# Ten of eleven row tiles of each half of a down projection through seven products, the plain parts moved ahead of the fourth product

## The chip, the cores and the metric

The kernel runs on one core of a Trainium2 chip. The metric is the device time of one execution in microseconds (us); the median of a few runs counts. Engines are named as in the profile: PE is the matrix engine, DVE the vector engine, ACT the scalar engine, POOL the GpSimd engine, SP the engine that issues most DMAs. A measurement of this kernel tells a difference from no change at about 0.2%, that is 2.2 us.

## The reference, cut to what matters

Two layers of a bidirectional encoder over 512 tokens with a model width of 1024. The change lies in the last line of each layer, the down projection with `w_down` (2816 x 1024).

```python
D_MODEL = 1024; SEQ = 512; DEPTH = 2; D_FF = 2816
def reference(...):
    for l in range(DEPTH):
        h = rmsnorm(x, mix_norm[l])
        ...                                   # attention, pooling and gating mixers
        x = x + jnp.einsum('bsn,nd->bsd', mix, w_o[l])
        h = rmsnorm(x, ffn_norm[l])
        g = jnp.einsum('bsd,df->bsf', h, w_gate[l])
        u = jnp.einsum('bsd,df->bsf', h, w_up[l])
        x = x + jnp.einsum('bsf,fd->bsd', jax.nn.silu(g) * u, w_down[l])
    return rmsnorm(x, final_norm)
```

## The kernel before

**Precision.** Every product of two float32 tiles is three matmuls: each operand is split into a high part (an ACT copy that rounds to the short type) and a low part (a DVE subtraction of the high part), and `mm` issues high x high, high x low, low x high. For weights `split` makes one `wu` tile of both parts out of a loaded 128x1024 tile `wr` (or `raw`); there are three `wu` buffers, so a split starts when the third `wu` before it has been used up on PE. For the left operand `halved` makes the two `xp` tiles.

**Seven products.** The activation is cut in two halves of 256 tokens (`i`) and two halves of the 2816 columns (`s`), the weight in two halves of rows (`h`) and two halves of 512 output columns (`s`). A product of 2x2 blocks by 2x2 blocks takes seven block products in place of eight (the Strassen-Winograd scheme). `products` issues them, `sum_of` builds the left operands (sums of activation blocks, tile names `xs` and `ac`), `operand` builds the right ones. The right operand of products 5, 6 and 4 is a running sum kept in `chain[b]`: W11, then + W12 (product 5), + W22 (product 6), + W21 (product 4). An addition to it is either a DVE addition of a second loaded tile (`wr<-wr,wr` in the profile) or `add_loaded`, a DMA issued from POOL that adds while it lands. Here W12 and W22 are added by DVE, W21 by DMA; product 7 has a DMA addition of its own (W22 onto a loaded W12). Product 3 uses the W22 tile that was loaded for product 6.

**Tiling.** Each half of the 2816 columns has eleven tiles of 128. Eight of them go through the seven products: `b` runs over four pairs of tiles, a "unit" here is one product and one pair: one 128x1024 weight split and twelve 128x512 matmuls (2 token blocks `j` x 2 tiles `kk` x 3). The last three tiles of each half are multiplied plainly in `rest`: `rest(1, ...)` for the second 512 output columns, `rest(0, ...)` for the first, each with three weight tiles, all three `wu` buffers, and 18 matmuls for each of four blocks of 128 tokens. The accumulating PSUM banks are `reg["z"]`, `reg["y"]`, `reg["x"]`, two each; `rest(1)` borrows two more, `spare`.

**Order.** The program order in `down` is product 1, 5, 6 and 3 interleaved by `b`, 2, 7, then `rest(1)`, product 4, `rest(0)`. A recording layer (`Program`) then places every instruction: `order` walks a list of ready instructions with planned times, `LEAD_FF = 100` lets loads and first uses of a buffer start up to 100 matmuls ahead of their place in the program. All instructions are emitted from one line, so the profile shows L493 for nearly all of them; they are told apart by the tile names.

**Ends.** A finished block of 128 tokens by 512 columns goes to `settle`. In layer 0 that is `back`: four PE transposes into a bank of tag `b` (two such banks, `spare` takes them too) and a DVE addition into `res`; `next_inputs` then prepares layer 1. In layer 1 it is `finish`: a square with a row sum (ACT), a gain (DVE), a power (POOL), two scalings (ACT and DVE) and the output DMAs.

Of the kernel before, what the change touches and what calls it, by code (L numbers as in the profile page):

```python
# [19 lines left out]
P = 128  # L20
# [59 lines left out]
def dn_unit(h, s, b):  # L80

    return 74 + (h * 8 + s * 4 if h < 2 else 16 + s * 3) + b
# [416 lines left out]
def encoder(ctx: ExitStack, tc: tile.TileContext, wts, xT, pos, cols, sgn, fin, cst, rc, out):  # L499
# [204 lines left out]
    for l in range(DEPTH):  # L704
# [560 lines left out]
        for c in range(3):  # L1265
# [3 lines left out]
            for mat in range(2):  # L1269
# [4 lines left out]
                def consume(src, j, i, s, c=c, w=w, nf=nf, mat=mat, stash=stash):  # L1274
# [25 lines left out]
                    for f in range(0, nf, 2):  # L1300
                        n = min(2, nf - f)
                        g, at = (s, 0) if f == 0 else ("both", s)
                        if g not in act:
                            act[g] = upool.tile([P, 2, T], F32, tag="u", name=nm("ac"), bufs=NU)
# [7 lines left out]
                        nc.scalar.copy(  # L1312
                            out=act[g][:, at : at + n, i * HALF : (i + 1) * HALF],
                            in_=ps[:, : n * HALF].rearrange("p (f q) -> p f q", q=HALF),
                        )
# [126 lines left out]
        sums = [None, None]  # L1442

        def sum_of(p, c):
            x11, x21, x12, x22 = (act[i, s, c] for s in range(2) for i in range(2))
            if p == 1:
                return x11
            if p == 2:
                return x12
            if p == 4:  # L1450
                return x22
            if p == 7:
                return x21
            if p == 5:
                sums[c] = upool.tile([P, 4, HALF], F32, tag="u", name=nm("xs"), bufs=NU)
# [10 lines left out]
        def operand(p, b):  # L1466
# [16 lines left out]
            chain["22"] = raw  # L1483
            add(chain[b][:], chain[b][:], raw[:])
            return chain[b]
# [3 lines left out]
        def products(ps_, due=None):  # L1489

            xs = {}
            for b in range(4):
                for p in ps_:
                    if b % 2 == 0:
                        xs[p] = halved(sum_of(p, b // 2))
                    xh, xl = xs[p]
                    wu = split(operand(p, b), U, nc.vector)
                    for j in range(2):
                        for kk in range(2):
                            k = 2 * b + kk  # L1500
                            js = slice(j * P, (j + 1) * P)
                            ws = slice(kk * T, (kk + 1) * T)
                            mm(
                                reg[REGION[p]][j][:], xh[:, k % 4, js], xl[:, k % 4, js], wu[:, 0, ws], wu[:, 1, ws],
                                p in OPENS and k == 0, k == 7,
                            )
                if due and b == 0:
                    settle(*due)

        KREST = [(1, 0), (1, 1), (0, 0), (0, 1), (0, 2), (1, 2)]  # L1510
        rest_parts = {}

        def rest_part(n):
            s, f = KREST[n]
            g = s if f < 2 else "both"
            if g not in rest_parts:
                m = U
                hi, lo = (upool.tile([P, 2, T], F32R, tag="u", name=nm("xp"), bufs=NU) for _ in range(2))
                nc.scalar.activation(flat(hi)[:, :m], flat(act[g])[:, :m], AF.Copy)
                add(flat(lo)[:, :m], flat(act[g])[:, :m], f32(flat(hi)[:, :m]), ALU.subtract)  # L1520
                rest_parts[g] = hi, lo
            return [x[:, f if f < 2 else s] for x in rest_parts[g]]

        def rest(h, targets, after):

            wus = [weights(l, dn_unit(2, h, b)) for b in range(3)]
            due = []
            for i, (banks, opens) in enumerate(targets):
                for j in range(2):
                    for k in range(6):  # L1530
                        xh, xl = rest_part(k)
                        t = 2 * i + j
                        js = slice(t * P, (t + 1) * P)
                        ws = slice(k % 2 * T, (k % 2 + 1) * T)
                        mm(
                            banks[j][:], xh[:, js], xl[:, js], wus[k // 2][:, 0, ws], wus[k // 2][:, 1, ws],
                            opens and k == 0, k == 5,
                        )
                    if due:
                        settle(*due.pop())  # L1540
                    due.append(after(i, j))
            return due.pop()
# [43 lines left out]
        def after0(i, j):  # L1586
            if i == 0:
                y = a1[j]
                add(y[:], reg["x"][j][:], y[:])
            else:  # L1590
                y = tmp()
                if last:
                    add(cols4(y[:]), cols4(reg["z"][j][:]), rows(2 + j, 0))
                else:
                    nc.scalar.copy(out=y[:], in_=reg["z"][j][:])
            return y, 2 * i + j, 0

        settle(*rest(0, [(reg["x"], False), (reg["z"], False)], after0))
# [19 lines left out]
def _pack(p):  # L1618
# [3 lines left out]
    for l in range(DEPTH):  # L1622
# [38 lines left out]
        for h in range(2):  # L1661
            for s in range(2):
                row += [wd[h, :8, :, s].transpose(1, 0, 2).reshape(P, -1)]
        for s in range(2):
            rest = [wd[h, 8 + f, :, s] for h, f in ((1, 0), (1, 1), (0, 0), (0, 1), (0, 2), (1, 2))]
            row += [np.stack(rest).transpose(1, 0, 2).reshape(P, -1)]
# [50 lines left out]
```

## Time and profile before

| | |
|---|---|
| median of 3 runs | 1096.61 us (1095.69 to 1096.83) |
| the profiled execution | 1096.24 us |
| its span, first to last instruction | 1094.5 us |
| mean granted clock of PE | 0.996 of full |
| PE busy | 1072.2 us, 98% of the span |
| DVE busy | 864.9 us, 79% |
| ACT busy | 649.7 us, 59% |
| POOL busy | 174.9 us, 16% |

The profiled execution lies within the three runs; what lies around its span is 1.74 us. Busy time is a share over stages with different limits, so the stages are read apart below.

### The profile page before, as it was taken

The numbers are of one execution on the slowest core, as the hardware profiler recorded it, in microseconds if no ns is written. First come the engines' busy times: TensorE is split into PE (matmuls) and PEld (weight loads), VectorE is DVE, ScalarE is ACT, GpSimd is POOL, SyncE is SP. The second block draws the span as 40 slices with busy tenths as digits, with TensorE's granted clock in tenths as the row PEclk, the third lists the DMA queues.
The fourth block names the chain that finished last, engine by engine and source line by source line (L and its number), as shares of the span: only waits on it lengthen the run. The fifth ranks groups of instructions, "written<-read, shape, count | busy, mean of one in ns | idle before, by whom it ended". The sixth has DMA issues, their size and how long they took to land.

```text
span 1094.5 us, 14564 instructions
## 1 busy us (share of the span) xinstructions
PE 1072.2 (98%) x5324; PEld 902.9 (82%) x5324; DVE 864.9 (79%) x1193; ACT 649.7 (59%) x993; POOL 174.9 (16%) x201
## 2 busy tenths in 40 slices
PE   9999899999999999999999999999999999999997
PEld 7787688888888899888887877888888889998885
DVE  7679996897877778995556898959977867799963
ACT  6357784775565556663443678747655655666632
POOL 0317430101001100030001263301001001100201
PEclk9999999999999999999999999999999999999999
DMA  6344313656545557392142533153767446563922
GB/s 214 101 119 117 104 39 128 219 153 135 155 130 120 122 132 248 114 235 80 60 132 67 140 99 88 58 229 99 187 141 169 109 117 142 130 219 102 259 64 96
DMA packets 45672, 146.90 MB, mean 134 GB/s; under 512 B 6000, under 2 KB 6256, under 8 KB 45600
## 3 DMA queue, kind: packets, MB, share of 16 engines
q1 hardware_dynamic: 35216, 112.24, 31.4%
q0 software_dynamic: 9808, 32.67, 17.0%
q10 hardware_dynamic: 576, 1.05, 0.3%
q8 instruction: 42, 0.69, 0.3%
q14 instruction: 30, 0.25, 0.1%
HBM read 135.33 MB, written 2.23 MB: 126 GB/s over the span
## 4 chain that ended last, share of the span: by engine, by line
PE 89%; DVE 4%; ACT 4%; DMA 1%; issue 1%; POOL 1%; POOLq 0%; SPq 0%; ACTq 0%; DVEq 0%
PE ps L493 89%; DVE u L493 2%; ACT t L493 1%; ACT u L493 1%; DMA wr<-in_wts 1%; DVE wu L493 1%; DVE s L493 1%; ACT wu L493 1%; DVE t L493 0%; POOL t L493 0%; DMA colt<-in_cols 0%; POOL z L493 0%; ACT vm L493 0%; DVE vz L493 0%; DVE wr L493 0%
## 5 line engine op out<-in xcount | busy, mean ns | idle before, releaser
L493 PE MATMUL ps<-wu,xp 128*128 128x512 f32 (+1 forms) x2976 | 657.7, 380 | 1.8 <-DVE wu L493 1.1
L493 PEld LDWEIGHTS ps<-wu,xp 128*128 128x128 f32 x2976 | 545.9, 188 | 92.8 <-DVE wu L493 2.3
L493 ACT ACTIVATE wu<-wr 128x1024 fp32r<-128x1024 f32 (+1 forms) x224 | 225.0, 1007 | 200.1 <-PE ps L493 163.5
L493 DVE TENSOR_TENSOR wu<-wr,wu 128x1024 fp32r<-128x1024 f32 (+1 forms) x224 | 257.9, 1154 | 89.6 <-ACT wu L493 88.5
L493 PE MATMUL ps<-u,wu 128*128 128x512 f32 x972 | 238.1, 397 | 2.8 <-DVE wu L493 2.1
L493 PEld LDWEIGHTS ps<-u,wu 128*128 128x128 f32 x972 | 180.1, 190 | 41.8 <-DVE wu L493 4.0
L493 POOL DMA_DIRECT2D wr<-in_wts x64 | 55.7, 978 | 553.0 <-DVE wr L493 276.6
L493 PE MATMUL ps<-u,u 128*128 128x256 f32 (+2 forms) x516 | 109.0, 349 | 5.2 <-ACT vm L493 1.7
L493 ACT ACTIVATE wu<-raw 128x1024 fp32r<-128x1024 f32 (+3 forms) x66 | 63.1, 959 | 65.5 <-PE ps L493 33.5
L493 PEld LDWEIGHTS ps<-u,u 128*128 128x128 f32 (+1 forms) x516 | 75.9, 190 | 21.0 <-DVE u L493 4.5
L493 ACT COPY t<-ps 128x512 f32<-128x512 f32 (+3 forms) x124 | 62.2, 502 | 49.3 <-PE ps L493 47.9
L493 DVE TENSOR_TENSOR wu<-raw,wu 128x1024 fp32r<-128x1024 f32 (+3 forms) x59 | 67.4, 1146 | 26.6 <-ACT wu L493 26.0
L493 DVE TENSOR_TENSOR wr<-wr,wr 128x1024 f32<-128x1024 f32 (+1 forms) x64 | 73.6, 1152 | 5.5 <-DMA wr<-in_wts 5.1
L493 DVE TENSOR_TENSOR u<-ps,u 128x512 fp32r<-128x512 f32 (+1 forms) x104 | 70.2, 683 | 6.1 <-ACT u L493 5.4
L493 DVE TENSOR_TENSOR t<-ps,t 128x512 f32<-128x512 f32 (+2 forms) x92 | 50.1, 566 | 24.6 <-PE ps L493 19.8
L493 ACT ACTIVATE u<-ps 128x512 fp32r<-128x512 f32 (+1 forms) x104 | 61.2, 595 | 12.1 <-PE ps L493 10.7
L493 ACT ACTIVATE t<-ps,s 128x512 f32<-128x512 f32 x64 | 43.9, 688 | 11.7 <-DVE s L493 11.2
L493 POOL TENSOR_SCALAR t<-t,s 128x512 f32<-128x512 f32 x55 | 38.4, 704 | 59.2 <-DVE s L493 48.4
L493 PE MATMUL ps<-ident,t 128*128 128x128 f32 x288 | 42.9, 274 | 0.8 <-DVE s L493 0.6
L493 DVE TENSOR_REDUCE s<-ps 128x1 f32<-128x512 f32 x64 | 42.9, 679 | 0.5 <-PE ps L493 0.2
L493 PEld LDWEIGHTS ps<-ident,t 128*128 128x128 f32 x288 | 34.2, 140 | 11.0 <-issue 3.2
L493 DVE TENSOR_TENSOR res<-ps,res 128x512 f32<-128x512 f32 x40 | 27.5, 686 | 18.9 <-PE ps L493 18.7
(130 smaller groups left out, 807.7 us busy)
## 6 DMA issues: line engine op xcount, KB each, us to landing
wr<-in_wts SPq DMA_DIRECT2D x104, 512.0 KB, 4.3
raw<-in_wts SPq DMA_DIRECT2D x50, 512.0 KB, 3.5
wr<-in_wts POOLq DMA_DIRECT2D x48, 512.0 KB, 5.6
wr<-in_wts SPq DMA_DIRECT2D x32, 384.0 KB, 3.1
wr<-in_wts POOLq DMA_DIRECT2D x16, 384.0 KB, 4.7
u<-u SPq DMA_DIRECT2D x16, 256.0 KB, 4.6
u<-u SPq DMA_DIRECT2D x32, 128.0 KB, 2.3
raw<-in_wts SPq DMA_DIRECT2D x8, 320.0 KB, 3.0
```

Source lines behind the costliest of these rows:

```text
L493: getattr(getattr(nc, op.engine), op.method)(*[real(x) for x in op.args], **{k: real(x) for k, x in op.kw.items()})
```

## The change

The number of row tiles of each half that go through the seven products rises from eight to ten, and the plain part falls from three tiles to one. So `b` runs over five units; the left operands of the fifth are 128x512 tiles, half as large, and both parts of one share a buffer. `rest` has one weight tile for each half of the columns. Both `rest(1)` and `rest(0)` now come ahead of product 4. The last two units of product 4 are issued together, first both for token block 0, then both for block 1 (`tails`), so that the two banks end twelve matmuls apart. The additions to `chain[b]` change place: W12 by DVE (product 5) as before, W22 by DMA (product 6, was DVE), W21 by DVE in product 2 (was a DMA in product 4), so that product 4 loads nothing. Product 3 loads W22 for itself. Counted over both layers in the built programs, PE has 24 matmuls fewer, DVE 28 instructions more, ACT 16 more, POOL 4 more, SP 2 more.

```diff
 def dn_unit(h, s, b):
-    return 74 + (h * 8 + s * 4 if h < 2 else 16 + s * 3) + b
+    return 74 + (h * 10 + s * 5 if h < 2 else 20 + s) + b
...
-        def halved(src):
-            hi, lo = (upool.tile([P, 4, HALF], F32R, tag="u", name=nm("xp"), bufs=NU) for _ in range(2))
+        def halved(src, n):
+            if n == 4:
+                hi, lo = (upool.tile([P, 4, HALF], F32R, tag="u", name=nm("xp"), bufs=NU) for _ in range(2))
+            else:
+                both = upool.tile([P, 4, HALF], F32R, tag="u", name=nm("xp"), bufs=NU)
+                hi, lo = both[:, :n], both[:, n : 2 * n]
             nc.scalar.activation(flat(hi), flat(src), AF.Copy)
             add(flat(lo), flat(src), f32(flat(hi)), ALU.subtract)
...
             if p == 1:
                 chain[b] = fetch(l, dn_unit(0, 0, b))
                 return chain[b]
-            if p == 2:
-                return fetch(l, dn_unit(1, 0, b))
+            if p == 6:
+                add_loaded(l, chain[b], dn_unit(1, 1, b))
+                return chain[b]
             if p == 4:
-                add_loaded(l, chain[b], dn_unit(1, 0, b))
                 return chain[b]
+            raw = fetch(l, dn_unit(1, 1, b) if p == 3 else dn_unit(1, 0, b) if p == 2 else dn_unit(0, 1, b))
             if p == 7:
-                raw = fetch(l, dn_unit(0, 1, b))
                 add_loaded(l, raw, dn_unit(1, 1, b))
-                return raw
-            if p == 3:
-                return chain["22"]
-            raw = fetch(l, dn_unit(0, 1, b) if p == 5 else dn_unit(1, 1, b))
-            chain["22"] = raw
-            add(chain[b][:], chain[b][:], raw[:])
-            return chain[b]
+            if p in (5, 2):
+                add(chain[b][:], chain[b][:], raw[:])
+            return chain[b] if p == 5 else raw
...
-            xs = {}
-            for b in range(4):
+            xs, tails = {}, []
+            for b in range(5):
                 for p in ps_:
                     if b % 2 == 0:
-                        xs[p] = halved(sum_of(p, b // 2))
+                        xs[p] = halved(sum_of(p, b // 2), 4 if b < 4 else 2)
                     xh, xl = xs[p]
                     wu = split(operand(p, b), U, nc.vector)
+                    tails.append((p, b, xh, xl, wu))
+                    if p == 4 and b == 3:
+                        continue
                     for j in range(2):
-                        for kk in range(2):
-                            k = 2 * b + kk
...
+                        for q, bb, xh, xl, wu in tails:
+                            for kk in range(2):
+                                k = 2 * bb + kk
...
+                    tails.clear()
...
-        def rest(h, targets, after):
-            wus = [weights(l, dn_unit(2, h, b)) for b in range(3)]
-            due = []
+        def rest(h, targets, after, due):
+            if not rest_parts:
+                rest_parts.extend(halved(act["both"], 4))
+            wu = weights(l, dn_unit(2, h, 0))
             for i, (banks, opens) in enumerate(targets):
                 for j in range(2):
-                    for k in range(6):
...
+                    for k in range(2):
+                        xh, xl = (x[:, 2 * k + i, j * P : (j + 1) * P] for x in rest_parts)
+                        ws = slice(k * T, (k + 1) * T)
+                        mm(banks[j][:], xh, xl, wu[:, 0, ws], wu[:, 1, ws], opens and k == 0, k == 1)
...
-        due = rest(1, [(reg["y"], False), (spare, True)], after1)
-        products([4], due)
...
+        due = []
+        rest(1, [(reg["y"], False), (spare, True)], after1, due)
+        rest(0, [(reg["x"], False), (reg["z"], False)], after0, due)
         if not last:
             next_inputs(1)
+        products([4])
...
-        settle(*rest(0, [(reg["x"], False), (reg["z"], False)], after0))
```

What this does to the order on the engines is shown at three places.

POOL, the additions by DMA in `down` of layer 1, before (the four of product 7, then the four of product 4; all write `wr` tiles):

```order
L493 DMA wr_9083<-in_wts 128x1024
L493 DMA wr_9105<-in_wts 128x1024
L493 DMA wr_9125<-in_wts 128x1024
L493 DMA wr_9146<-in_wts 128x1024
L493 DMA wr_8667<-in_wts 128x1024
L493 DMA wr_8679<-in_wts 128x1024
L493 DMA wr_8710<-in_wts 128x1024
L493 DMA wr_8746<-in_wts 128x1024
```

And after the change (the five of product 6 onto `chain`, then the five of product 7):

```order
L493 DMA wr_8688<-in_wts 128x1024
L493 DMA wr_8700<-in_wts 128x1024
L493 DMA wr_8731<-in_wts 128x1024
L493 DMA wr_8767<-in_wts 128x1024
L493 DMA wr_8761<-in_wts 128x1024
L493 DMA wr_9221<-in_wts 128x1024
L493 DMA wr_9239<-in_wts 128x1024
L493 DMA wr_9261<-in_wts 128x1024
L493 DMA wr_9282<-in_wts 128x1024
L493 DMA wr_9311<-in_wts 128x1024
```

The additions to `chain` have moved from behind those of product 7 to ahead of them, and there is one more in each group.

PE, the plain parts of layer 0 after the change (`ps_4184`, `ps_4198` are the `y` banks, `ps_4510` is `x` of block 0, `ps_4721`, `ps_4744` are `spare`, the 128x128 rows by `ident` are the transposes of `back`):

```order
L493 MATMUL ps_4198<-wu_4655,xp_4560 128x512
L493 MATMUL ps_4510<-wu_4672,xp_4546 128x512
L493 MATMUL ps_4715<-ident,t_4475 128x128 x4
L493 MATMUL ps_4721<-wu_4655,xp_4546 128x512 x2
...
L493 MATMUL ps_4736<-ident,t_4497 128x128 x4
L493 MATMUL ps_4510<-wu_4672,xp_4560 128x512
L493 MATMUL ps_4744<-wu_4655,xp_4546 128x512 x2
...
L493 MATMUL ps_4752<-ident,t_4285 128x128 x4
```

Before, eighteen matmuls stood between one group of transposes and the next; now six stand there, with a few of `rest(0)` put in between.

PE, the last rows of the program after the change (`ps_8799`, `ps_8814` are the two `z` banks, `wu_9593` and `wu_9612` the last two units of product 4):

```order
L493 MATMUL ps_8799<-wu_9593,xp_9434 128x512 x2
L493 MATMUL ps_8799<-wu_9593,xp_9440 128x512
L493 MATMUL ps_8799<-wu_9593,xp_9434 128x512 x2
L493 MATMUL ps_8799<-wu_9593,xp_9440 128x512
L493 MATMUL ps_8799<-wu_9612,xp_9457 128x512 x6
L493 MATMUL ps_8814<-wu_9593,xp_9434 128x512 x2
L493 MATMUL ps_8814<-wu_9593,xp_9440 128x512
L493 MATMUL ps_8814<-wu_9593,xp_9434 128x512 x2
L493 MATMUL ps_8814<-wu_9593,xp_9440 128x512
L493 MATMUL ps_8814<-wu_9612,xp_9457 128x512 x6
```

The two banks that end last are twelve matmuls apart; before, the last two ended eighteen apart, at the end of `rest(0)`.

## Rows read from the trace of the kernel before

**Rows 1.** The page, part 1: busy us, share of the span, instructions.

```profile
PE 1072.2 (98%) x5324; PEld 902.9 (82%) x5324; DVE 864.9 (79%) x1193; ACT 649.7 (59%) x993; POOL 174.9 (16%) x201
```

**Rows 2.** The chain that ended last, in order: start us, us, what.

```profile
412.62 99.85 PE ps L493 x477
512.48 0.70 DVE t L493
513.23 92.80 PE ps L493 x458
...
952.25 134.62 PE ps L493 x643
1086.90 0.70 DVE t L493
```

**Rows 3.** Busy time by stage, down of layers 0 and 1; columns in the first line.

```profile
core 0: us, PE busy (x) PEld busy (x) DVE busy (x) ACT busy (x) POOL busy (x), PEclk, DMA share, GB/s
433.00:547.00 114.00, 113.65 (x518) 93.66 (x517) 89.14 (x90) 59.49 (x69) 9.31 (x15) 1.00 0.47 125
974.00:1086.90 112.90, 112.86 (x514) 92.59 (x512) 89.48 (x97) 59.83 (x76) 9.83 (x11) 1.00 0.46 126
```

**Rows 4.** Timeline of PE, end of down in layer 0; waits in brackets.

```profile
512.28 0.60 PE L493 MATMUL ps<-ident,t 128*128 128x128 f32 x4
513.23 4.38 PE L493 MATMUL ps<-wu,xp 128*128 128x512 f32 x18 [0.35 <-DVE t L493]
```

**Rows 5.** Timeline of DVE, end of down in layer 1.

```profile
1082.82 0.69 DVE L493 TENSOR_TENSOR t<-ps,res 128x512 f32<-128x512 f32 x1 [0.90 <-PE ps L493]
...
1085.50 0.49 DVE L493 TENSOR_SCALAR t<-t,s 128x512 f32<-128x512 f32 x1 [0.44 <-POOL s L493]
1086.90 0.69 DVE L493 TENSOR_TENSOR t<-ps,res 128x512 f32<-128x512 f32 x1 [0.91 <-PE ps L493]
```

**Rows 6.** Timeline of ACT at the same end.

```profile
1085.50 0.73 ACT L493 ACTIVATE t<-t,s 128x512 f32<-128x512 f32 x1 [1.23 <-POOL s L493]
1086.02 0.34 ACTq L493 DMA_DIRECT2D out_dram<-t  x1
```

**Rows 7.** Timeline of DVE in products 5 to 7 of layer 0.

```profile
442.08 1.22 DVE L493 TENSOR_TENSOR wr<-wr,wr 128x1024 f32<-128x1024 f32 x1
443.21 1.22 DVE L493 TENSOR_TENSOR xs<-ac,ac 128x1024 f32<-128x1024 f32 x1
444.35 1.22 DVE L493 TENSOR_TENSOR wu<-wr,wu 128x1024 fp32r<-128x1024 f32 x1
...
492.68 1.23 DVE L493 TENSOR_TENSOR wu<-wr,wu 128x1024 fp32r<-128x1024 f32 x1 [1.49 <-ACT wu L493]
```

**Rows 8.** The page, part 5: weight splits on ACT and DVE.

```profile
L493 ACT ACTIVATE wu<-wr 128x1024 fp32r<-128x1024 f32 (+1 forms) x224 | 225.0, 1007 | 200.1 <-PE ps L493 163.5
L493 DVE TENSOR_TENSOR wu<-wr,wu 128x1024 fp32r<-128x1024 f32 (+1 forms) x224 | 257.9, 1154 | 89.6 <-ACT wu L493 88.5
```

**Rows 9.** Timeline of DVE in the plain part of layer 0: PSUM reads.

```profile
512.48 0.69 DVE L493 TENSOR_TENSOR t<-ps,t 128x512 f32<-128x512 f32 x1 [3.28 <-PE ps L493]
513.09 0.68 DVE L493 TENSOR_TENSOR res<-ps,res 128x512 f32<-128x512 f32 x1
```

**Rows 10.** Timeline of POOL, the additions by DMA in layer 0.

```profile
466.51 0.86 POOL L493 DMA_DIRECT2D wr<-in_wts  x1 [52.79 <-DVE wr L493]
...
476.82 0.87 POOL L493 DMA_DIRECT2D wr<-in_wts  x1 [7.15 <-DMA wr<-in_wts]
477.90 4.43 POOL L493 DMA_DIRECT2D wr<-in_wts  x5 [0.21 <-issue]
```

**Rows 11.** DMA issues starting in us 466, 476, 482 and 1024: us to landing.

```profile
wr<-in_wts POOLq DMA_DIRECT2D x1, 512.0 KB, 5.2
wr<-in_wts POOLq DMA_DIRECT2D x1, 512.0 KB, 7.2
wr<-in_wts POOLq DMA_DIRECT2D x1, 512.0 KB, 16.7
wr<-in_wts POOLq DMA_DIRECT2D x1, 512.0 KB, 20.1
```

More of the change, by code (lines that the diff above doesn't have):

```diff
@@ L1301, in consume @@
                         n = min(2, nf - f)
-                        g, at = (s, 0) if f == 0 else ("both", s)
+                        g = s if f == 0 else "both"
                         if g not in act:
-                            act[g] = upool.tile([P, 2, T], F32, tag="u", name=nm("ac"), bufs=NU)
+                            act[g] = upool.tile([P, 4, HALF], F32, tag="u", name=nm("ac"), bufs=NU)
                         ps = bank("b")
@@ L1440, in halved @@
             return hi, lo
-        sums = [None, None]
+        sums = [None] * 3
         def sum_of(p, c):
-            x11, x21, x12, x22 = (act[i, s, c] for s in range(2) for i in range(2))
+            x11, x21, x12, x22 = (
+                act[i, s, c] if c < 2 else act[s][:, 2 * i : 2 * i + 2] for s in range(2) for i in range(2)
+            )
             if p == 1:
@@ L1454, in sum_of @@
             if p == 5:
-                sums[c] = upool.tile([P, 4, HALF], F32, tag="u", name=nm("xs"), bufs=NU)
+                sums[c] = upool.tile([P, 4, HALF], F32, tag="u", name=nm("xs"), bufs=NU)[:, : x11.shape[1]]
                 add(flat(sums[c]), flat(x21), flat(x22), ALU.subtract)
@@ L1498, in products @@
                     for j in range(2):
-                        for kk in range(2):
-                            k = 2 * b + kk
[L1501 to L1506, printed above, removed]
-                if due and b == 0:
-                    settle(*due)
@@ L1510, in encoder @@
[L1510 to L1522, printed above, removed]
@@ L1524, in rest @@
-        def rest(h, targets, after):
-            wus = [weights(l, dn_unit(2, h, b)) for b in range(3)]
-            due = []
+                        for q, bb, xh, xl, wu in tails:
+                            for kk in range(2):
+                                k = 2 * bb + kk
+                                js = slice(j * P, (j + 1) * P)
+                                ws = slice(kk * T, (kk + 1) * T)
+                                mm(
+                                    reg[REGION[q]][j][:], xh[:, k % 4, js], xl[:, k % 4, js], wu[:, 0, ws],
+                                    wu[:, 1, ws], q in OPENS and k == 0, k == 9,
+                                )
@@ L1528, in rest @@
+                    tails.clear()
+                if due and b == 0:
+                    settle(*due.pop())
+        rest_parts = []
+        def rest(h, targets, after, due):
+            if not rest_parts:
+                rest_parts.extend(halved(act["both"], 4))
+            wu = weights(l, dn_unit(2, h, 0))
             for i, (banks, opens) in enumerate(targets):
                 for j in range(2):
-                    for k in range(6):
[L1531 to L1538, printed above, removed]
+                    for k in range(2):
+                        xh, xl = (x[:, 2 * k + i, j * P : (j + 1) * P] for x in rest_parts)
+                        ws = slice(k * T, (k + 1) * T)
+                        mm(banks[j][:], xh, xl, wu[:, 0, ws], wu[:, 1, ws], opens and k == 0, k == 1)
+                    y = after(i, j)
@@ L1539, in rest @@
                     if due:
                         settle(*due.pop())
-                    due.append(after(i, j))
-            return due.pop()
+                    if y:
+                        due.append(y)
         a1, u1, v5 = {}, {}, {}
@@ L1580, in encoder, with after0 @@
             add(v5[j][:], v5[j][:], reg["z"][j][:], ALU.subtract)
-        due = rest(1, [(reg["y"], False), (spare, True)], after1)
-        products([4], due)
+        def after0(i, j):
+            if i == 0:
+                add(a1[j][:], reg["x"][j][:], a1[j][:])
+                return a1[j], j, 0
+        due = []
+        rest(1, [(reg["y"], False), (spare, True)], after1, due)
+        rest(0, [(reg["x"], False), (reg["z"], False)], after0, due)
         if not last:
             next_inputs(1)
[L1586 to L1589, printed above, removed]
-            else:
[L1591 to L1596, printed above, removed]
-        settle(*rest(0, [(reg["x"], False), (reg["z"], False)], after0))
+        products([4])
+        for j in range(2):
+            y = tmp()
+            if last:
+                add(cols4(y[:]), cols4(reg["z"][j][:]), rows(2 + j, 0))
+            else:
+                nc.scalar.copy(out=y[:], in_=reg["z"][j][:])
+            settle(y, 2 + j, 0)
         if not last:
@@ L1662, in _pack @@
             for s in range(2):
-                row += [wd[h, :8, :, s].transpose(1, 0, 2).reshape(P, -1)]
+                row += [wd[h, :10, :, s].transpose(1, 0, 2).reshape(P, -1)]
         for s in range(2):
-            rest = [wd[h, 8 + f, :, s] for h, f in ((1, 0), (1, 1), (0, 0), (0, 1), (0, 2), (1, 2))]
-            row += [np.stack(rest).transpose(1, 0, 2).reshape(P, -1)]
+            row += [wd[:, 10, :, s].transpose(1, 0, 2).reshape(P, -1)]
         layers.append(np.concatenate(row, axis=1))
```

2 lines of the change are left out of this document (1 added, 1 removed).

## The prediction

> **What bounds the kernel now.** I read the page's first part, then the chain of waits, then the busy time by stage, then single timelines where the change touches them. The first part has PE busy for 98% of the span [rows 1]. The chain shows what that means in the two `down` stages: one run of PE work up to 512.48, a DVE addition of 0.70, another run of 92.80 that goes far into layer 1, and at the other end a run of 134.62 that stops only when the last bank of the kernel is done, at 1086.90 [rows 2]. [...] So PE's queue is full there, the one wait is the 0.35 us ahead of a matmul in [rows 4], and a matmul that disappears shortens the stage by its own distance to the next. A matmul that other engines can't feed in time would lengthen it.
>
> That distance is read from the end: the last two banks are eighteen 128x512 matmuls apart, and the DVE additions that wait for them start at 1082.82 and 1086.90 [rows 5]. 4.08 / 18 = 0.2267 us. (The profile's mean of one matmul is longer, since matmuls overlap; it isn't used.) [...]
>
> **What is removed.** Per layer the seven products had 7 products x 4 units x 12 = 336 matmuls and the plain part 2 x 4 blocks x 18 = 144, together 480. Now they have 7 x 5 x 12 = 420 and 2 x 4 x 6 = 48, together 468. Twelve fewer per layer, 24 in all: 24 x 0.2267 = **5.44 us** off PE. Transposes and everything outside `down` stay as they are.
>
> **What is added on DVE and ACT, and why I cost it at nothing.** In DVE operations of 128x1024 per layer: splits 34 to 37, additions to `chain` 8 to 10, left parts 17 to 18.5 (a 128x512 counts half), sums of activations 8 to 10. That is 8.5 more. Back to back they start 1.135 us apart (442.08, 443.21, 444.35 in [rows 7]), so 9.6 us more per layer on DVE; ACT gets 3 splits and 1.5 left parts of about 1.0 us [rows 8], 4.5 us. The cover is PE's own time: 468 x 0.2267 = 106 us of matmuls, against 89 + 10 on DVE and 60 + 5 on ACT [rows 3]. On average that holds, but DVE runs without a gap through product 5 and after, until it waits for ACT at 492.68 [rows 7], so the order in time matters. A unit takes PE 12 x 0.2267 = 2.72 us. I count DVE operations from the start of product 1 on:
>
> - Before, to the end of product 5: 6 + 14 = 20, 22.7 us of DVE for 8 units, 21.8 us of PE: short by 0.9. To the end of 6 and 3: 40, 45.4 us for 43.5: short by 1.9. To the end of 2: 46, 52.2 for 54.4.
> - Now, to the end of product 5: 7.5 + 17.5 = 25, 28.4 us for 10 units, 27.2 us of PE: short by 1.2. To the end of 6 and 3: 45, 51.1 for 54.4: 3.3 to spare. To the end of 2: 57.5, 65.3 for 68.0.
>
> The worst shortage before was 1.9 us, and work ahead of time (up to 100 matmuls, 22.7 us) covered it, since PE waited for nothing there. The worst now is 1.2. If none of the added work were covered, it would cost 9.6 us a layer; I take 0.
>
> **What is moved.** W22 in product 6 now comes by a DMA from POOL that adds onto `chain[b]`. It may start when product 5 has split that tile and must be there when product 6 splits it. From the split of unit b in product 5 to that in product 6 lie 5 + b units, 13.6 us for the first and 24.5 for the last. Of this, issuing takes 0.86 [rows 10], landing 5.2 when it is alone [rows 11], and the split on ACT and DVE about 2.4 with its signals [rows 8]: 8.5 of 13.6. In a row of six, the first landed 7.2 after 476.82 and the last 16.7 after about 482.3, at 499.0 [rows 10, 11]: 3.0 us for each, a little more than the 2.72 at which product 5 will ask for them. So the fifth lands some 1.1 us later after its request than the first (4 x 0.28), with 10.9 us more time. Hidden, with 5 us to spare at the tightest. What is queued behind these DMAs on POOL is only product 7's additions, which now share the queue with no additions for product 4. Product 4 loads nothing, and the loads of the others have 22.7 us of lead, more than the longest landing of [rows 11]. I take 0.
>
> **The plain part of layer 0.** Only six matmuls (1.36 us) stand between the blocks that `back` has to transpose, and its transposes and `spare` share two banks. A bank comes free after a DVE read of PSUM, 0.69 long and some 0.6 apart from the next [rows 9], behind whatever DVE has in its queue. Laying the new order of PE and DVE side by side at these distances, PE waits at three places: about 0.28 ahead of the second group of transposes, 0.07 ahead of the second `spare` block, 0.4 ahead of the sixth group. That is 0.75 in place of the 0.35 of [rows 4]: **+0.4 us**. The bounds: nothing (-0.35), or each of the six groups as long as the one of [rows 4] (2.1, +1.75). The value lies near the row's. In layer 1 `finish` uses no bank, and I see no wait.
>
> **The end.** The last two banks are now 2.72 us apart, not 4.08. After the first, DVE's last operation on that block runs from 2.68 to 3.17 us after its first (1082.82 to 1085.50 in [rows 5]) and stands ahead of the last bank's addition in the order; that addition starts about **0.4 us** late. ACT is free by 3.54 [rows 6], before the late addition has ended. Bounds 0 and 0.5.
>
> **Sum.** 1096.24 - 5.44 + 0.4 + 0.4 = 1091.6 against the profiled execution. That one is 0.37 below the median of the runs, so the median becomes **1092.0 us**, 0.42% less.
>
> **Rivals.**
>
> 1. *DVE falls short in product 5.* Per layer product 5 asks DVE for 17.5 operations, 19.9 us, in 13.6 us of PE: 6.3 to be done ahead, where it was 15.9 in 10.9, 5.0. If the 1.3 more aren't found ahead of time, PE waits 1.3 in each layer: 1092.0 + 2.6 = 1094.6, no difference that can be measured. For it: DVE has no gap there [rows 7]. Against it: product 1 is a unit longer too and leaves DVE 5.1 us where it left 4.1, and the shortage counted over both products is smaller than one that was covered.
> 2. *The additions by DMA come late in product 6 (slower).* It decides from a landing of 10.3 us for the first: each microsecond beyond that is a microsecond of PE in each layer, and beyond 12.6 the gain is gone; 16 gives 1092.0 + 2 x 5.7 = 1103.4. For it: 16.7 and 20.1 were seen [rows 11]. Against it: these were the last of a row, issued within 6 us, and here each waits for its own split. [...]
> 3. *No price at the seams.* The waits of the plain part and the late addition cost nothing: 1096.61 - 5.44 - 0.35 = 1090.8. It is the lower part of my own case.
>
> **How the numbers follow.** My case, with its bounds (rival 3 below; 1.75 and 0.5 at the seams above, 1093.4), has a chance of 0.87. Rival 1 has 0.09 and rival 2 0.04. A measurement tells 0.2%, 2.2 us, so my case is faster, rival 1 the same, rival 2 slower. The range goes from 1090.4 (rival 3 and a little of the runs' spread) to 1094.4, just short of rival 1.
>
> **What would show it.** In the profile after, PE busy falls by 5.4 us; in the stretches of `down` it stays within 1 us of the stretch, 24 matmuls fewer. DVE waits for ACT again by the end of product 2. The waits of PE in the plain part of layer 0 add up to under 1 us, and from the last matmul to the end of the span there is 0.4 us more than the 7.6 of before. It is wrong if PE waits for DVE in product 5, or for the split of an added `wr` tile in product 6 (ACT waiting for a DMA from POOL), or if matmuls in the new order lie further apart than 0.2267.

## The result and the profile after

The changed kernel took 1090.95 us (median of 4 runs, 1090.54 to 1091.58), the kernel before 1096.72 beside it (4 runs). The measured ratio is 0.9941 [0.9922, 0.9960], faster (the two medians alone give 0.9947). Two later measurements of the same two kernels gave 0.9958 [0.9946, 0.9970] and 0.9951 [0.9937, 0.9964]. The mean of the three, 0.9950, is 5.5 us; the forecast's 0.42% was 4.6. The first ratio puts the time at 0.9941 x 1096.61 = 1090.1, below the forecast range (1090.4 to 1094.4); the three medians by themselves (1090.95, 1092.86, 1091.65) lie in it. Two executions among those below are left out of every comparison: the profiled one of r4 (1515.52 us, at a mean granted clock of 0.654) and one of the kernel before (2756.72 us).

The page after, part 1, answers to [rows 1]:

```profile
PE 1065.7 (98%) x5300; PEld 897.9 (82%) x5300; DVE 882.8 (81%) x1221; ACT 660.0 (61%) x1009; POOL 178.9 (16%) x205
```

PE has 24 matmuls fewer and is busy 6.5 us less, where the forecast said 5.4. DVE got 17.9 us more (forecast 2 x 9.6), ACT 10.3 more (2 x 4.5). The chain that ended last, as in [rows 2]:

```profile
412.03 189.85 PE ps L493 x927
...
949.88 128.87 PE ps L493 x619
1078.74 0.02 issue
1078.77 0.70 DVE t L493
```

The break at 512.48 of [rows 2] is gone: one run of PE goes from the end of `gate`/`up` in layer 0 through the whole of `down` and into layer 1. To size this I read each `down` stage between two events that both kernels have: from the start of the last group of four transposes of `mg` (the activation) to the first matmul with `ones` in layer 0, and to the end of PE's last matmul in layer 1. These are the PE rows of the changed kernel at those places:

```profile
434.88 0.60 PE L493 MATMUL ps<-ident,mg 128*128 128x128 f32 x4
...
565.29 0.95 PE L493 MATMUL ps<-ones,acc 128*128 128x1 f32 x8
...
972.78 0.60 PE L493 MATMUL ps<-ident,mg 128*128 128x128 f32 x4
...
980.78 100.67 PE L493 MATMUL ps<-wu,xp 128*128 128x512 f32 x443
```

Layer 0 takes 565.29 - 434.88 = 130.41 us and layer 1 980.78 + 100.67 - 972.78 = 108.67. The kernel before has 569.34 - 435.47 = 133.87 and 982.84 + 104.03 - 975.09 = 111.78. So the stages give 3.46 and 3.11, and 12 matmuls are only 2.72 in each. The two other parts of the span differ too, in both directions: the start up to the first event by -0.59, the stretch between the stages by +1.74, though the order of instructions there is the same in both kernels.

The windows of the two stages, first of after (columns as in [rows 3]), then of before:

```profile
434.88:565.29 130.41, 130.41 (x593) 107.81 (x592) 108.06 (x116) 71.62 (x88) 10.96 (x17) 1.00 0.52 141
972.78:1081.85 109.07, 108.67 (x497) 89.62 (x495) 97.36 (x109) 63.99 (x82) 11.19 (x13) 1.00 0.54 148
```

```profile
435.47:569.34 133.87, 133.52 (x606) 110.14 (x605) 98.62 (x102) 67.19 (x81) 9.31 (x15) 1.00 0.46 126
975.09:1086.90 111.81, 111.77 (x509) 91.75 (x507) 88.39 (x95) 59.53 (x75) 9.83 (x11) 1.00 0.46 128
```

PE is busy for the whole of its stage after as before, at a granted clock of 1.00, while DVE went from 98.62 to 108.06 us in layer 0 and from 88.39 to 97.36 in layer 1. The added work of DVE, 9 us a layer, is hidden.

The seams of the plain part in layer 0 answer to [rows 4]. PE's timeline after:

```profile
518.11 0.60 PE L493 MATMUL ps<-ident,t 128*128 128x128 f32 x4
518.46 2.57 PE L493 MATMUL ps<-wu,xp 128*128 128x512 f32 x10
520.87 0.66 PE L493 MATMUL ps<-ident,t 128*128 128x128 f32 x4
521.28 1.85 PE L493 MATMUL ps<-wu,xp 128*128 128x512 f32 x7
522.97 0.60 PE L493 MATMUL ps<-ident,t 128*128 128x128 f32 x4
523.32 0.95 PE L493 MATMUL ps<-wu,xp 128*128 128x512 f32 x3
```

Read start to start, a group of transposes takes 0.35 us, once 0.41 (520.87 to 521.28). In [rows 4] the same distance is 513.23 - 512.28 = 0.95. So the wait there was 0.6 us. The bracket in that row says 0.35, because it counts from the modelled end of the transposes. The timeline of weight loads (PEld), before and after, shows the wait of [rows 4] and a small one that is left:

```profile
513.23 3.95 PEld L493 LDWEIGHTS ps<-wu,xp 128*128 128x128 f32 x18 [0.58 <-DVE t L493]
```

```profile
520.87 0.42 PEld L493 LDWEIGHTS ps<-ident,t 128*128 128x128 f32 x4 [0.28 <-DVE res L493]
```

The load at 520.87 waits for DVE's read of a bank, ahead of the second group of transposes. From start to start it costs PE about 0.1 us: 0.06 in the group, and 0.03 in the ten matmuls ahead of it, against the other rows.

The end answers to [rows 5]. DVE's timeline after:

```profile
1078.77 0.69 DVE L493 TENSOR_TENSOR t<-ps,res 128x512 f32<-128x512 f32 x1 [2.74 <-PE ps L493]
...
1081.45 0.49 DVE L493 TENSOR_SCALAR t<-t,s 128x512 f32<-128x512 f32 x1 [0.44 <-POOL s L493]
1081.85 0.68 DVE L493 TENSOR_TENSOR t<-ps,res 128x512 f32<-128x512 f32 x1
```

PE ends at 1081.45; the last addition starts at 1081.85, 0.40 behind it (0.03 before), after the `TENSOR_SCALAR` of the block before. That is the forecast's term, and the reason that it gave.

DVE waits for ACT again at 500.13, within product 2 (eight of the 300 matmuls of products 1, 5, 6, 3 and 2 lie ahead of 435.23, the others end at about 501.5); before it was 492.68 [rows 7]. The five additions by DMA of product 6 in layer 0 (three of the five in POOL's timeline, then the time to landing over the five):

```profile
444.74 0.87 POOL L493 DMA_DIRECT2D wr<-in_wts  x1 [31.60 <-DMA wr<-in_wts]
448.15 0.86 POOL L493 DMA_DIRECT2D wr<-in_wts  x1 [2.54 <-DVE wu L493]
450.42 0.87 POOL L493 DMA_DIRECT2D wr<-in_wts  x1 [1.41 <-DVE wu L493]
```

```profile
DMA to landing us min/median/max: 6.6/7.8/8.4
```

They are issued as each split of product 5 ends, 2.3 to 3.4 us apart, and land in 6.6 to 8.4, under the 10.3 that the forecast could bear (layer 1: 5.5 to 9.2). No split of product 6 waits for them. DVE has no wait of 0.2 us from 436 to 499, and an issue takes 0.87 us there (0.86 in [rows 10]).

### The profile page after: what moved, and what is told of

It is laid out like the page before. It is cut to its first block, busy times and chain, and to the rows that moved or that the text cites. A ratio compares the mean times of both kernels' runs of the same rounds, so it can differ in the third digit from the quotient of the medians.

```text
span 1089.8 us, 14605 instructions
## 1 busy us (share of the span) xinstructions
PE 1065.7 (98%) x5300; PEld 897.9 (82%) x5300; DVE 882.8 (81%) x1221; ACT 660.0 (61%) x1009; POOL 178.9 (16%) x205
## 4 chain that ended last, share of the span: by engine, by line
PE 86%; DVE 6%; ACT 3%; DMA 2%; issue 1%; POOL 1%; SPq 0%; POOLq 0%; DVEq 0%; ACTq 0%
PE ps L493 86%; DVE u L493 2%; ACT u L493 1%; ACT t L493 1%; DVE wu L493 1%; DMA wr<-in_wts 1%; DVE t L493 1%; DVE s L493 1%; ACT wu L493 1%; DMA res<-in_xT 0%; POOL t L493 0%; DMA raw<-in_wts 0%; POOL z L493 0%; DVE vz L493 0%; ACT vm L493 0%
## 5 line engine op out<-in xcount | busy, mean ns | idle before, releaser
L493 ACT ACTIVATE wu<-wr 128x1024 fp32r<-128x1024 f32 (+1 forms) x238 | 240.4, 1011 | 212.0 <-PE ps L493 170.4
L493 DVE TENSOR_TENSOR wu<-wr,wu 128x1024 fp32r<-128x1024 f32 (+1 forms) x238 | 275.3, 1158 | 92.8 <-ACT wu L493 91.6
L493 POOL DMA_DIRECT2D wr<-in_wts x68 | 59.1, 869 | 587.4 <-DVE wr L493 250.0
L493 ACT ACTIVATE wu<-raw 128x1024 fp32r<-128x1024 f32 (+3 forms) x58 | 54.6, 945 | 56.6 <-PE ps L493 29.0
L493 DVE TENSOR_TENSOR wr<-wr,wr 128x1024 f32<-128x1024 f32 (+1 forms) x68 | 78.2, 1155 | 6.3 <-DMA wr<-in_wts 5.8
L493 DVE TENSOR_TENSOR wu<-raw,wu 128x1024 fp32r<-128x1024 f32 (+3 forms) x51 | 56.5, 1111 | 24.1 <-ACT wu L493 23.7
L493 ACT ACTIVATE t<-ps,s 128x512 f32<-128x512 f32 x64 | 43.9, 688 | 11.7 <-DVE s L493 11.2
L493 ACT COPY ac<-ps 128x512 f32<-128x512 f32 (+1 forms) x48 | 25.8, 549 | 23.1 <-PE ps L493 21.8
```

The costliest lines, as they stand in the source:

```text
L493: getattr(getattr(nc, op.engine), op.method)(*[real(x) for x in op.args], **{k: real(x) for k, x in op.kw.items()})
```

## Two theories and twelve runs

**Theory A** is the forecast's: the time follows the matmuls that PE no longer does, and what DVE, ACT and the DMA queues get besides is hidden. **Theory B**: what feeds PE counts as well, so that a part of the gain stands or falls with where the additions to `chain` are done. **Theory C**: the place of the plain parts counts. Later runs name theories of their own. The table gives each run's ratio to the kernel before and, from its trace, the two stages as above and the end, from PE's last matmul to the end of the last store's issue on ACT. From there to the end of the span it takes 3.99 to 4.06 us in the three traces with eight tiles, 4.32 to 4.39 in six of the eight with ten (the changed kernel's three among them), and 3.67 (r11), 5.19 (r9), 4.71 (r7) and 5.69 (r8) in the others. No run says why, so that part is left out of the table.

| run | ratio [95%] | layer 0 | layer 1 | end | sum |
|---|---|---|---|---|---|
| before | | 133.87 | 111.78 | 3.57 | 249.22 |
| changed, first | 0.9941 [0.9922, 0.9960] | 130.41 | 108.67 | 3.99 | 243.07 |
| changed, second (r1) | 0.9958 [0.9946, 0.9970] | 130.76 | 108.71 | 3.99 | 243.46 |
| changed, third (r12) | 0.9951 [0.9937, 0.9964] | 130.52 | 108.69 | 3.99 | 243.20 |
| r2 `rest(0)` last | 0.9962 [0.9950, 0.9974] | 130.38 | 108.68 | 4.86 | 243.92 |
| r10 no stagger (r4: 0.9960) | 0.9948 [0.9931, 0.9965] | 130.56 | 108.67 | 4.30 | 243.53 |
| r3 old additions | 0.9988 [0.9979, 0.9998] | 130.59 | 110.76 | 4.00 | 245.35 |
| r11 the same, 4's by DVE | 0.9946 [0.9927, 0.9964] | 130.63 | 108.71 | 4.10 | 243.44 |
| r5 new additions alone | 0.9991 [0.9978, 1.0004] | 134.10 | 111.86 | 3.57 | 249.53 |
| r6 plain parts first, alone | 1.0007 [0.9996, 1.0017] | 134.24 | 112.76 | 4.30 | 251.30 |
| r7 all eleven | 0.9972 [0.9961, 0.9984] | 129.84 | 112.22 | 4.11 | 246.17 |
| r8 all eleven, 5's by DMA | 0.9961 [0.9948, 0.9973] | 129.64 | 109.62 | 4.10 | 243.36 |
| r9 changed, 5's by DMA | 0.9944 [0.9925, 0.9964] | 130.53 | 108.74 | 3.98 | 243.25 |

### r1, the changed kernel again

> The changed kernel itself, unchanged, beside the others on one chip. Theory A (24 matmuls fewer give 5.4 us, some 1.0 us of short PE waits in the plain parts of before is gone, the late last addition costs 0.4): 5.5 to 6.3 us less than before. Theory B (the additions to the running weight sum that changed place are worth something of their own) and theory C (the place of the plain parts is) expect the same here. If the time inside the span differs from run to run by about 1 us while the down stages stay, the rest was spread of other stages.

1092.86 us against 1096.87; 0.42% [0.30, 0.54] faster, the forecast's 4.6 us. The stages agree with the first trace within 0.4 us, yet this profiled execution has a span of 1093.9 where the first had 1089.8. The difference lies ahead of the stages: the first event comes at 438.80, not 434.88. PE's timeline at the end of `gate`/`up` in layer 0, here and (second fence) in the kernel before, then a window of r1 right behind the wait (columns as in [rows 3]):

```profile
413.36 0.45 PE L493 MATMUL ps<-wu,xp 128*128 128x384 f32 x1 [1.80 <-ACT wu L493]
414.36 9.50 PE L493 MATMUL ps<-wu,xp 128*128 128x384 f32 x44 [0.55 <-DVE wu L493]
```

```profile
411.62 0.44 PE L493 MATMUL ps<-wu,xp 128*128 128x384 f32 x1 [0.28 <-ACT wu L493]
```

```profile
415.00:418.40 3.40, 3.40 (x12) 3.40 (x11) 1.13 (x2) 1.27 (x3) 0.46 (x1) 0.50 0.63 103
```

One weight split comes late there by 0 to 1.8 us from execution to execution, in code that the change doesn't touch. In r1, after that wait and one of 0.55, the granted clock is 0.50 for these 3.4 us, and the row of 44 matmuls takes 9.50 us where it took 7.90 in the first trace. A span thus moves by more than the change's terms, and the stages are the finer measure.

### r2 and r4/r10, the order at the end

r2 is the changed kernel with `rest(0)` behind product 4 as before and without the stagger; r4 and r10 leave only the stagger out (second fence).

```diff
-        rest(0, [(reg["x"], False), (reg["z"], False)], after0, due)
+        products([4], due)
...
-        products([4])
...
+        rest(0, [(reg["x"], False), (reg["z"], False)], after0, due)
```

```diff
-                    if p == 4 and b == 3:
-                        continue
```

> Ten of eleven tiles, but the second plain part stands behind product 4 as before, and product 4 is not staggered; the same 24 matmuls fewer. Theory A: 5.0 to 6.2 us less than before, since one weight tile instead of three leaves PE nothing to wait for wherever the plain part stands; the last two banks end six matmuls (1.36 us) apart, so the last addition may start up to 1 us late. Theory C: 3.5 to 4.6 us less.

> The changed kernel without the staggered end of product 4: the last two banks end six matmuls (1.36 us) apart instead of twelve. Theory A: 5.2 to 6.2 us less than before, the part from the last matmul to the end of the span between equal and 0.8 us longer than in the changed kernel. Anything over 1 us lost would say that the stagger carries part of the gain.

> The changed kernel without the staggered end of product 4, once more, for its trace. If the stagger does what it looks like: stages of 130.4 to 130.8 and 108.7 us as in the changed kernel, and a tail from PE's end to the span's end of 8.6 to 9.2 us where the changed kernel has 8.35; the median within 0.1% of the changed kernel's. If the stagger also costs something in the products: a shorter stage in layer 1 by 0.3 us or more.

r4 left no trace to compare; r10 is the same kernel again. The stages of r2 and r10 are the changed kernel's, to 0.2 us (r1's layer 0 apart). The end differs: 3.57 before, 4.86 with `rest(0)` last (two blocks come 1.36 us apart and DVE is 0.8 late), 4.30 with the plain parts first, 3.99 with the stagger too. So the order gives 0.56 us back and the stagger 0.31, of the 1.29 that the end would have lost. The stagger costs nothing in the products. None of this is large enough for the ratios to tell: r2's 0.38% is 4.2 us and r4's 0.40% is 4.4, outside the ranges of theory A, and r2's is in that of theory C, but the changed kernel beside them gave only 4.6. By the stages r2 has the whole gain, and theory C falls.

### r3 and r11, the additions as before

r3 is the changed kernel with `operand` of the kernel before: W22 in product 6 by a load and a DVE addition (product 3 shares its tile), W21 in product 4 by a DMA from POOL. r11 is r3 with product 4's addition by a load and DVE:

```diff
             if p == 4:
-                add_loaded(l, chain[b], dn_unit(1, 0, b))
+                raw = fetch(l, dn_unit(1, 0, b))
+                add(chain[b][:], chain[b][:], raw[:])
                 return chain[b]
```

> Ten of eleven tiles and the new order of the plain parts, but the running weight sum is built as before: W22 by DVE in product 6, W21 by a DMA in product 4, product 3 uses the tile of product 6. Counted as in the prediction, DVE is then short by 2.3 us at the end of products 6 and 3 (50 operations x 1.135 = 56.7 against 54.4 of PE), where 1.9 was covered before. Theory A: 4.5 to 6.2 us less than before, at most 0.4 to 0.8 a layer lost to DVE. Theory B: 3.5 us less or smaller.

> The run with the old additions, with product 4's additions by a load and DVE in place of a DMA from POOL. Theory D (the old additions lost their 3 us because ten additions by DMA stood in a row from 1026.9 to 1045.3, beside loads that took 18.6 and 21.8 us to land): the waits for DMA in product 7 go, the stage of layer 1 falls from 110.8 to 108.7, the median to 0.4% under the kernel before. Theory E (W22's addition by DVE in product 6 asks too much of DVE): nothing changes in products 5, 6 and 3; 0.1% under the kernel before as it was.

r3 keeps 0.12% [0.02, 0.21]: theory B. Its layer 1 is 2.1 us longer than the changed kernel's. That is less than the 3 to 5 us by which the ratios differ; where the rest lies isn't shown. POOL's timeline in r3, the DMA issues from 985 on, and ACT and PE near the end of product 7:

```profile
1026.89 0.87 POOL L493 DMA_DIRECT2D wr<-in_wts  x1 [73.94 <-DVE wu L493]
1028.26 1.76 POOL L493 DMA_DIRECT2D wr<-in_wts  x2 [0.50 <-issue]
1031.50 1.76 POOL L493 DMA_DIRECT2D wr<-in_wts  x2 [1.48 <-DMA wr<-in_wts]
1037.18 1.76 POOL L493 DMA_DIRECT2D wr<-in_wts  x2 [3.92 <-DMA wr<-in_wts]
1045.28 2.65 POOL L493 DMA_DIRECT2D wr<-in_wts  x3 [6.34 <-DVE wu L493]
```

```profile
wr<-in_wts SPq DMA_DIRECT2D x13, 512.0 KB, 3.8
wr<-in_wts POOLq DMA_DIRECT2D x10, 512.0 KB, 15.1
raw<-in_wts SPq DMA_DIRECT2D x2, 512.0 KB, 20.2
```

```profile
1049.93 1.06 ACT L493 ACTIVATE wu<-raw 128x1024 fp32r<-128x1024 f32 x1 [2.11 <-DMA raw<-in_wts]
...
1054.32 1.06 ACT L493 ACTIVATE wu<-wr 128x1024 fp32r<-128x1024 f32 x1 [3.32 <-DMA wr<-in_wts]
...
1055.43 7.24 PE L493 MATMUL ps<-wu,xp 128*128 128x512 f32 x30 [0.59 <-ACT wu L493]
```

The additions of products 7 and 4, ten now, are issued within 21 us, some in twos and threes, and land in 15.1 (median); two loads beside them take 20.2 (14.4 in the changed kernel). ACT waits 3.32 us for one tile, and PE for ACT: from start to start PE loses 2.0 us between 1054 and 1064. The changed kernel's additions, five and five, land in 8.0. r11 shows that this accounts for the loss: with product 4's five off the queue (the same bytes now come by SP's loads), layer 1 is back at 108.71 and the ratio at 0.9946, though DVE now does every addition but product 7's. Theory D holds; DVE had room for W22 in product 6.

### r5 and r6, parts of the change alone

r5 is the kernel before (eight tiles) with the new `operand`, r6 the kernel before with both plain parts ahead of product 4:

```diff
         due = rest(1, [(reg["y"], False), (spare, True)], after1)
-        products([4], due)
+        settle(*due)
...
-        settle(*rest(0, [(reg["x"], False), (reg["z"], False)], after0))
+        rest(0, [(reg["x"], False), (reg["z"], False)], after0)
+        products([4])
```

> The kernel before with nothing but the new places of the additions to the running weight sum (W22 by DMA in product 6, W21 by DVE in product 2, product 3 loads W22 itself). No matmul fewer. Theory A: within 0.7 us of before. Theory B: 1.5 us or more below before.

> The kernel before, eight of eleven tiles, with both plain parts ahead of product 4 and nothing else. No matmul fewer. Theory A: between 1 us less and 1 us more than before, for the three weight tiles of each plain part still hold all weight buffers. Theory C: 1 us or more below before.

Neither brings anything: 0.9991 [0.9978, 1.0004] and 1.0007 [0.9996, 1.0017]. Both keep the wait of [rows 4] in layer 0 (0.35 in its bracket, stages of 134.10 and 134.24). r6 is 0.73 longer at the end and 0.98 in layer 1. So neither part has a gain of its own without the ten tiles, and the wait of [rows 4] went with them, not with the new order: r2 has ten tiles and the old place of `rest(0)`, and its layer 0 is 130.38.

### r7 and r8, all eleven tiles

r7 sends the eleventh tile through the products as half a unit, and there is no plain part: 18 matmuls fewer per layer than before. Finished blocks are then settled during products 2, 7 and 4. r8 takes product 5's additions off DVE:

```diff
-            if p == 6:
-                add_loaded(l, chain[b], dn_unit(1, 1, b))
+            if p in (5, 6):
+                add_loaded(l, chain[b], dn_unit(p - 5, 1, b))
                 return chain[b]
```

> All eleven tiles of each half through the seven products, no plain part: 7 x 5.5 x 12 = 462 matmuls a layer in place of 468, so 12 fewer than the changed kernel over both layers. The eleventh tile is a half unit (512 columns of weights, 128x256 left parts). Theory A: 2.7 us less than the changed kernel, 8.0 to 9.0 us less than before, as long as DVE (short by 1.3 us at the end of product 5, counted as in the prediction) keeps up. If DVE or the longer row of additions by DMA becomes the limit: 6 us less than before or smaller, with PE waiting in products 5 to 3.

> All eleven tiles through the products, and product 5's additions to chain also by DMA from POOL in place of a load and a DVE addition: six DVE operations less per layer between products 1 and 5. Theory S (with all eleven, DVE falls short in product 5 of layer 1; the three waits of PE of 1.15, 1.17 and 1.23 us are that): the waits go, the stage of layer 1 falls from 112.2 to between 108.0 and 108.7, the median to 0.6 to 0.7% under the kernel before. Theory Q (what limits is the row of additions by DMA): twelve in a row at about 3.0 us each are 36 us, for 30 us of PE in products 1 and 5; ACT waits for DMA wr, PE waits 2 to 6 us in each layer, and the median is level with the kernel before or above it.

18 x 0.2267 x 2 would be 8.2 us less; r7 gains 0.28% [0.16, 0.39], some 3 us. Layer 0 has its share (129.84, 4.03 less), layer 1 has none. PE's timeline there, and DVE's share of the stretch (columns as in [rows 3]):

```profile
1022.34 0.73 PE L493 MATMUL ps<-wu,xp 128*128 128x512 f32 x2 [1.15 <-ACT wu L493]
1024.25 2.56 PE L493 MATMUL ps<-wu,xp 128*128 128x512 f32 x10 [1.17 <-DVE wu L493]
1028.04 40.21 PE L493 MATMUL ps<-wu,xp 128*128 128x512 f32 x176 [1.23 <-DVE xp L493]
```

```profile
1009.00:1031.00 22.00, 18.45 (x79) 14.30 (x78) 21.71 (x25) 10.80 (x12) 0.00 (x0) 1.00 0.46 145
```

DVE works 21.71 of 22.00 us and PE waits three times, 3.55 us by the brackets and 4.4 from start to start: rival 1 of the forecast, DVE short behind product 5, one step further than the change goes. With product 5's additions by DMA (r8) these three waits are gone and layer 1 falls by 2.6 to 109.62, as theory S said, but not to the 108.0 to 108.7 that it gave, and the gain is 0.39% where it gave 0.6 to 0.7. New waits stand in product 7:

```profile
1056.67 0.73 PE L493 MATMUL ps<-wu,xp 128*128 128x512 f32 x2 [0.70 <-ACT wu L493]
1057.93 6.64 PE L493 MATMUL ps<-wu,xp 128*128 128x512 f32 x28 [0.52 <-DVE wu L493]
```

Here ACT's split comes behind two scalings of `finish` (ACT at 1053.79 and 1054.95, the split at 1055.58). With a third wait ahead of product 4 these cost PE 2.2 us from start to start, most of the 2.7 that the twelve matmuls fewer than the changed kernel's would save; that the scalings are the cause is read from the order on ACT, no run moved them. Why layer 0, with the same products, has no waits of that size behind product 5 wasn't tested.

### r9, the changed kernel with product 5's additions by DMA

The edit is r8's, with ten tiles.

> The changed kernel with product 5's additions by DMA as in the run of all eleven. Theory S: DVE isn't short in the changed kernel, so taking five operations off it brings nothing: 0.4 to 0.5% under the kernel before, the two down stages and the tail 247.4 to 247.9 us together. Theory Q: ten additions in a row are 30 us for 27 us of PE, so the last come late and PE waits 1 to 3 us a layer: 0.0 to 0.2% under the kernel before.

0.9944 [0.9925, 0.9964] and a sum of 243.25: as the changed kernel. With ten tiles DVE isn't short, and taking five operations off it in each layer brings nothing. Theory Q falls: ten additions one after the other, each waiting for its split, cost PE nothing, with landings of 7.9 to 11.2 us in layer 0 (the nine from 435.31 on). The expectation's own sum, with the time to the end of the span, is 248.4 and misses its 247.4 to 247.9; the excess lies behind the last store's issue (5.19 us, 4.34 to 4.39 in the changed kernel).

### r12, the changed kernel a third time

> The changed kernel a third time, for the size of the gain. Reading of the traces so far (24 matmuls at 0.2267 us, 0.6 us of a stall in layer 0 and 0.4 us of two small waits in layer 1 gone, 0.4 us later at the end): 6.0 us, 0.54 to 0.55% under the kernel before; layer 0's stage 130.4 to 130.8 us, layer 1's 108.6 to 108.8. The forecast's own sum (no stall gone, 0.4 us added at the seams): 4.6 us, 0.42%.

0.49% [0.36, 0.63]: between the two readings, and the interval holds both. The stages of the trace (130.52, 108.69) are those of the first reading. The timed runs alone don't settle 4.6 against 6.0 us; the stages speak for 6.0 in the stages.

## Where the prediction was right, and which step failed

**The matmuls: right.** 5324 became 5300. The 365 matmuls from 435.23 to 518.11 start 0.2271 us apart, so 24 are 5.45 us, where the forecast had 0.2267 and 5.44 (in the kernel before the profile's mean of one is 392 ns).

**The added work at nothing: right.** DVE and ACT got the amounts that were counted, and PE is busy for the whole of its stages. r9 shows that DVE has room, r7 that the room ends at the next step.

**The additions by DMA in product 6: right**, with landings of 5.5 to 9.2 us for the 10.3 allowed. What the forecast passed over is that product 4's additions have to leave POOL's queue: it counted the queue behind product 7 as emptier, but not what it would have been with ten tiles and the old additions. By r3 against the changed kernel that is at least 0.3% of the time.

**The plain part of layer 0, +0.4: this step failed.** It put three waits of 0.75 us together in place of "the 0.35 of [rows 4]". The seven traces with ten tiles other than r3's have layer 0 shorter by 3.11 to 3.49, mean 3.33: 0.61 more than the matmuls, where the forecast had 0.4 less. (The kernel before has one trace, 133.87; r5 and r6, with its eight tiles, have 134.10 and 134.24.) Both sides of the term were off. The wait before was 0.6, to be read from start to start in the same two rows. And of the 0.75 laid out for the new order about 0.1 came: the load ahead of the second group, the first place that the forecast named, waits 0.28 for DVE and costs PE a third of that, and the other two waits show in no row. The order has 10, 7, 3, 3 and 6 matmuls between the groups of transposes.

**Layer 1, "I see no wait": half right.** There are none after. But the kernel before had some, which the rows of PE don't show. Its timeline of weight loads (PEld):

```profile
1005.02 44.99 PEld L493 LDWEIGHTS ps<-wu,xp 128*128 128x128 f32 x199 [0.32 <-DVE wu L493]
1059.51 13.49 PEld L493 LDWEIGHTS ps<-wu,xp 128*128 128x128 f32 x60 [0.21 <-DVE wu L493]
1073.19 6.90 PEld L493 LDWEIGHTS ps<-wu,xp 128*128 128x128 f32 x31 [0.20 <-DVE wu L493]
```

Three times a weight load waited for a split of DVE. The first is in products 6 and 3, where the forecast counted DVE as short by 1.9 and took it as covered. The second is at the first unit of product 4, right behind `rest(1)`, the third in `rest(0)`. DVE's splits there waited for ACT's, and at the third ACT waited for a load:

```profile
1058.23 1.22 DVE L493 TENSOR_TENSOR wu<-wr,wu 128x1024 fp32r<-128x1024 f32 x1 [1.36 <-ACT wu L493]
...
1070.83 1.06 ACT L493 ACTIVATE wu<-raw 128x1024 fp32r<-128x1024 f32 x1 [1.92 <-DMA raw<-in_wts]
```

In the changed kernel the row of weight loads runs from 980.75 to the end without a wait. Layer 1 is shorter by 3.04 to 3.11 (the same seven), 0.36 more than the matmuls. The brackets add up to 0.73, but from start to start the matmuls at these places (1004.73, 1005.02 and 1005.36; 1059.56 and 1059.85; 1073.26 and 1073.53) lie only 0.27 further apart than 0.2267 each. That these waits are most of the 0.36 is read from the rows; no run took them away alone.

**The end, +0.4: right up to the last store's issue**, 3.99 for 3.57. From PE's end to the end of the span, which the forecast gave as its sign, it is 8.35 for 7.6: 0.3 more came behind that issue, and no run says why.

**The sum.** -5.44 - 0.61 - 0.36 + 0.42 is -6.0 in the stages, and the three traces of the changed kernel give -6.15, -5.76 and -6.02; the forecast had -4.64. So the forecast was too high by two terms, the plain part of layer 0 (by 1.0) and layer 1 (by 0.36). Timed, the three ratios give -6.5, -4.6 and -5.4. With the 0.3 behind the last issue the stages give -5.7; what is left to the timed mean of -5.5 is within the spread outside: the stretch between the two stages takes 405.2 to 407.7 us in kernels with ten tiles, and 405.8 to 406.2 in the three with eight. Whether it is a little longer with ten tiles stays open. That the first ratio, and not the other two, puts the time outside the range is spread: the stages of the three traces agree to 0.4 us.

## What to carry to other kernels

Read the size of a wait from start to start of the matmuls, and look in the weight loads' rows for where one may be: a bracket on PE gave 0.35 for a wait of 0.6, and the 0.7 us of brackets on loads in layer 1, which cost PE 0.27, stood only with the loads. Ask of a step that is moved what it would do if it stayed: here the moved additions gave nothing alone, but left where they were they cost at least 3 of the 5 us. Where an engine off the critical path is hidden at 90% of a stage, count its work product by product, since one half step more (eleven tiles for ten) can make it the bound.

## What the runs showed of the hardware

- Additions by DMA (512 KB onto SBUF) land in 5.5 to 9.2 us when five are issued some 2.7 us apart (the changed kernel, product 6), in 7.9 to 11.2 when it is ten (r9, layer 0, the nine from 435.31 on), and in 15.1 (median) when ten come in twos and threes with loads beside them (r3).
- Each time a group of transposes stands between matmuls, the row of matmuls behind it takes some 0.10 to 0.17 us more in all than its count times 0.2267 (521.28 to 522.97: 1.69 for seven), in both kernels.
- The stores of 256 KB at the end land in a median of 2.4 us on SP's queue and of 2.0 on ACT's (the kernel before, the changed kernel, r1, r9 and r11, from 1080 on), but the span ends 3.7 to 5.7 us after the last issue: 4.34 to 4.39 in three executions of the changed kernel.
